# Second feed-forward: eight sums of output weights made in DRAM beside its first product

## The chip, the cores and the metric

The kernel runs on one core of one Trainium2 chip. The metric is the device time of one execution in microseconds. Its engines are TensorE (PE in the profile, with its weight loads as PEld), VectorE (DVE), ScalarE (ACT), GpSimd (POOL) and SyncE (SP), which here only issues DMAs. GpSimd issues DMAs too: those that add to what stands at their destination.

## What is computed

One decoder layer on 512 tokens of width 1024, all in float32. Two feed-forwards stand around a token mixer, each between two RMS norms; the feed-forward's inner width is 2816.

```python
def swiglu_ffn(x, w_in, w_out):
    gate, up = jnp.split(x @ w_in, 2, axis=-1)
    return (jax.nn.silu(gate) * up) @ w_out

x = x + 0.5 * rms_norm(swiglu_ffn(rms_norm(x, norm_pre[l, 0]), ffn1_w_in[l], ffn1_w_out[l]), norm_post[l, 0])
mixed = token_mixer(rms_norm(x, norm_pre[l, 1]), w_mix_in[l], ..., w_mix_out[l])
x = x + rms_norm(mixed, norm_post[l, 1])
x = x + 0.5 * rms_norm(swiglu_ffn(rms_norm(x, norm_pre[l, 2]), ffn2_w_in[l], ffn2_w_out[l]), norm_post[l, 2])
```

The token mixer has two groups of recurrent heads (HGRN2 and mLSTM) that read columns of one projection. The change touches only how one operand of the second feed-forward's second product, `ffn2_w_out`, is prepared.

## The kernel before

**Precision.** Every operand of a large product is split into a high part (a rounded copy) and a low part (what the copy lost), and a product is three passes on TensorE: high by high, high by low, low by high. For a block of weights the split is `split` (line 271): ScalarE makes the high part (line 294), VectorE subtracts it to get the low one (line 296). `feed` (line 332) keeps up to four split blocks ahead of TensorE.

**Stages, in order of time.** The first feed-forward has its first product (`ffn_in`, line 843) and its second (`ffn_out`, line 964); then come the mixers (`mixer`, line 1778, with jobs of projection that fill TensorE between the steps of the recurrences); then the second feed-forward through the same two functions, with `self.second` true.

**Seven products for eight.** Blocks of a feed-forward's first product are multiplied by a scheme of seven products for a 2 by 2 block, so quarters of weights must be added to one another. There are 11 pairs of inner blocks with seven products each (some blocks of the second feed-forward are done ahead in another way). In the first product these sums are made on VectorE (line 310, a few on GpSimd). `ORDER2` is the second feed-forward's order of 76 products, written out by hand; its first 14 are made by `ffn_head`, and `ffn_in` loops over the other 62 with index n. One product is 24 matmuls of 256 columns.

**Loads.** `weights` (line 207) fixes for each load the index at which it is due: when its ring of buffers (`raw`, three deep, or `raw2`, five deep) has a free place, and not more than eight blocks before its first use. `load_due` (line 236) issues it on SP's queue (line 255). SP takes its queue in order, so a load that waits for a buffer holds up whatever stands behind it.

**Sums of the output weights, in DRAM.** In the second product some inner blocks are "quartered", that is also done with seven products for eight: eight of them in the first half of the output columns and five (first feed-forward) or seven (second) in the second half. The sums of output weights that they need are not made on an engine but in DRAM, one item for each quartered block, by `sums_ahead` (line 932). An item is a generator of four steps: three copies from `ffn2_w_out` into a tile `f2sums` on SP's queue, put behind the newest weight load (lines 938 to 940; 128, 128 and 256 KB); then three DMAs of GpSimd that add to the tile (line 944; 256, 128 and 128 KB), one in each step, each waiting for what it reads. The sum is later loaded like a weight.

`sums_due(f, n, done)` (line 947) sets which items are still to do: those from `done` to `n` in the order of the dictionary. `make_sums` (line 956), at each call, starts one more item and takes every started one a step further. So one item takes four calls, and m items take m + 3 calls.

The 15 items of the second feed-forward, before: the copies of the first seven (`EARLY`) are issued at the end of the first feed-forward by `copies_early`, and their adds come in the mixers, behind GpSimd's making of masks. The next six, up to `AHEAD` = 13, are made in the mixers: `job_f` (for `conv0` to `conv3`) and `job_t` (for `hi` and `mv`) call `make_sums` 12 times. The last two are made in the first half of the second product, where `ffn_out` calls `make_sums` after every other block, six times. The first feed-forward makes its own 13 items differently: from n = 15 on in its `ffn_in`, every fifth product (`EVERY`), ten calls, and the rest in `ffn_out`.

The order of instructions on each engine comes from the program's order and a planner's modelled times; `behind` (line 513) ties an instruction behind another one of its engine.

Of the kernel before, what the change touches and what calls it, by code (L numbers as in the profile page):

```python
# [91 lines left out]
PLACES, LATER = {2: 1, 4: 2, 6: 0, 8: 3}, {7: (2, 3)}  # L92

AGAIN, ROWS = (10,), (18, 19, 20, 21)
EVERY, EARLY, AHEAD = 5, 7, 13

# [25 lines left out]
class Layer:  # L124
# [718 lines left out]
    def ffn_in(self):  # L843

        nc = self.nc
        if not self.second:
            self.begun = ()
            self.sums_due("f1")
        for n, (p, t) in enumerate(ORDER2[len(HEADS2) :] if self.second else ORDER[len(HEADS) :]):
            if n > 14 and n % EVERY == 0 and not self.second:  # L850
                self.make_sums()
            if n == 14 and self.second:

                with self.behind(self.pooled):
                    nc.gpsimd.drain()
            with self.behind(*(self.c22 if p in ("p3", "p5") and self.second else ())):
                self.feed()
            self.c22 = []
            self.lag()
            self.prod(p, t)  # L860
            self.after(p, t)
            if t == PAIRS - 1 and p in ("p3", "p7"):
                self.hs.append(self.h_tile(len(self.hs)))
            if n == 1 and not self.second:
                self.lower_bound()
        self.feed()
        self.lag()
# [96 lines left out]
    def ffn_out(self, gpost_row, scale, after, trans, head):  # L964
# [89 lines left out]

        with self.behind(*([self.loaded] if self.second else [])):
            g = self.gain("gpost", gpost_row)
        if self.second:
            self.sums_due("f2", done=AHEAD)
        n = 0
        for half in range(2):  # L1060
            C = [[self.ps() for _ in range(2)] for _ in range(2)]
# [716 lines left out]
    def mixer(self):  # L1778
        nc, tc = self.nc, self.tc
        self.got, self.jobs = set(), deque()  # L1780
        self.sums_due("f2", AHEAD, EARLY)
        with tc.tile_pool(name="ma", bufs=1) as ma:
            self.vh = ma.tile([P, NT, NH, P], F32, name="vh")
            self.qk = ma.tile([P, NT, T], F32, name="qk")
            self.sT = ma.tile([P, 16, P], F32, name="sT")
            self.qd = ma.tile([P, NH, 3 * P], F32, name="qd")
            self.kdt = ma.tile([P, NH, 3 * P], F32, name="kdt")
            self.S = self.kdt.rearrange("p h (c v) -> p h c v", v=P)
            self.eend = ma.tile([P, 16], F32, name="eend")
            with tc.tile_pool(name="mb", bufs=1) as mb:  # L1790
                self.mb = mb
                kes = [mb.tile([P, NT, P], F32, name=f"ke{n}") for n in range(2)]
                self.q = [mb.tile([P, 2, T], F32, tag="q", bufs=2, name=f"q{p}") for p in range(2)]
                self.xr1 = ma.tile([P, 2, D], F32R, tag="vm", bufs=1, name="xr1")
                self.xr = {}
                qps = {}
                for n in range(NH):
                    self.jobs.append(self.job_f(f"hq{n}", lambda ps, n=n: qps.__setitem__(n, ps)))
                for n in range(4):
                    self.jobs.append(self.job_f(f"conv{n}", lambda ps, n=n: self.conv(n, ps)))  # L1800
                self.jobs.append(self.job_rows())
                self.jobs.append(self.job_t("hi", lambda i, ps: nc.scalar.copy(self.vh[:, i].rearrange("p h v -> p (h v)"), ps), self.xr))
                self.jobs.append(self.job_t("mv", lambda i, ps: self.values_mv(ma, i, ps)))

                with tc.issue_after(self.pow.ins):
                    self.gate_weights(ma, mb)
                self.forget_gates(mb)
                with tc.issue_after(self.pow.ins):
                    nc.gpsimd.memset(self.sT, 0.0)
                    self.masks(ma, mb)  # L1810
                self.until("hq3")
                for n in range(NH):
                    nc.scalar.activation(self.q[n // 2][:, n % 2], qps[n], AF.Silu)
                self.hgrn_levels(0, kes, FILL[0])
                self.until("rows")
                nc.scalar.activation(self.qk, self.qk, AF.Silu)
                self.hgrn_levels(1, kes, FILL[1], self.gate_rows(ma))
            with tc.tile_pool(name="mc", bufs=1) as mc:
                self.y = mc.tile([P, NT, D], F32, name="y")
                self.jobs.append(self.job_t("hg", lambda i, ps: nc.scalar.activation(self.y[:, i, :W], ps, AF.Silu)))  # L1820
                self.until("hi")
                self.spread_maxima()
                self.hgrn_states()
                self.mlstm_scores(mc)
                self.jobs.append(self.job_t("mo", self.gate_mo))
                self.chunks(self.mlstm_values, FILL[2])
                self.until("hg")
                self.chunks(self.hgrn_values, FILL[3])
                self.until("mo")
                for i in range(NT):  # L1830
                    self.to_t(i, self.y[:, i], (0,))
                self.mix_out0()
# [145 lines left out]
```

## Time and profile before

| | |
|---|---|
| median of three runs | 915.06 us (914.81 to 915.23) |
| the profiled execution | 914.82 us, span 913.1 us |
| mean granted clock of TensorE | 0.999 |
| HBM read, written | 143.20 MB, 31.48 MB |
| first product of the first feed-forward, about | 12 to 223 us |
| mixers, about | 340 to 585 us |
| first product of the second feed-forward, about | 585 to 800 us |
| its second product, about | 795 to 907 us |

A row of a group gives line, engine, operation, the tile written and the tiles read, shapes, count, and then busy time and mean duration of one; a row of one line or tile gives the shortest, median and longest duration in ns and the first and last start. A wait row gives who waited, for what, and the total in us, the times and the longest. "PEq", "SPq" and so on are the engines' queues, which issue DMAs and wait.

### The profile page before, as it was taken

What the parts mean: (1) busy time and instruction counts of PE and PEld (TensorE: products, weight loads), DVE (VectorE), ACT (ScalarE), POOL (GpSimd) and SP (SyncE); (2) the same over time, 40 slices, a digit from 0 to 9 for tenths busy, and PEclk for the clock granted to TensorE, in tenths of its full rate; (3) what the DMA queues carried; (4) which work ended last, traced back from release to release, by engine and by line L of the source; (5) the groups of instructions that cost most, each with busy time, mean ns of one, the idle gap of its engine ahead of it and who ended that gap; (6) DMA issues with size and microseconds to landing.
All of it is one profiled execution on the core that took longest, in us unless ns stands there. A gap on an engine that the chain in (4) does not pass through costs nothing.

```text
span 913.1 us, 18148 instructions
## 1 busy us (share of the span) xinstructions
PE 904.7 (99%) x7330; PEld 874.7 (96%) x7330; DVE 767.1 (84%) x1005; ACT 522.3 (57%) x749; POOL 183.2 (20%) x256
## 2 busy tenths in 40 slices
PE   9999999999999999999999999999999999999997
PEld 8999999999999999998888888899999999999997
DVE  6899988889888876699986655699899889988886
ACT  7645545557566557857643345694445545757661
POOL 2541112121111047742230300313000000010002
PEclk9999999999999999999999999999999999999999
DMA  9355779775897825899953127053354445388542
GB/s 311 83 161 140 186 191 213 188 156 137 222 273 237 249 62 143 158 200 210 204 119 116 40 76 253 24 162 95 97 156 140 139 130 156 101 238 242 171 144 93
DMA packets 127921, 146.51 MB, mean 160 GB/s; under 512 B 16335, under 2 KB 100303, under 8 KB 127837
## 3 DMA queue, kind: packets, MB, share of 16 engines
q1 hardware_dynamic: 111868, 130.14, 46.8%
q0 software_dynamic: 15680, 14.69, 11.8%
q8 instruction: 57, 0.93, 0.4%
q10 hardware_dynamic: 288, 0.52, 0.2%
q14 instruction: 28, 0.22, 0.1%
HBM read 143.20 MB, written 31.48 MB: 191 GB/s over the span
## 4 chain that ended last, share of the span: by engine, by line
PE 62%; ACT 0%; DVE 0%; DVEq 0%; POOLq 0%; issue 0%; POOL 0%; ACTq 0%
PE ps L619 23%; PE ps L1012 8%; PE ps L549 6%; PE ps L198 5%; PE ps L200 5%; PE ps L199 5%; PE ps L1004 4%; PE ps L560 1%; PE ps L1441 1%; PE ps L364 1%; PE ps L1540 0%; PE ps L1742 0%; PE ps L1491 0%; PE ps L1715 0%; PE ps L1739 0%; PE ps L1505 0%
## 5 line engine op out<-in xcount | busy, mean ns | idle before, releaser
L294 ACT CAST w<-raw 128x1024 fp32r<-128x1024 f32 x246 | 250.9, 1027 | 190.6 <-PE ps L619 91.7
L296 DVE TENSOR_TENSOR w<-raw,w 128x1024 fp32r<-128x1024 f32 x246 | 299.4, 1221 | 30.7 <-ACT w L294 29.5
L619 PE MATMUL ps<-xq,w 128*128 128x256 f32 x2016 | 236.9, 277 | 0.0
L619 PEld LDWEIGHTS ps<-xq,w 128*128 128x128 f32 x2016 | 232.8, 188 | 0.0
L619 PE MATMUL ps<-sq,w 128*128 128x256 f32 x1512 | 177.6, 276 | 0.0
L619 PEld LDWEIGHTS ps<-sq,w 128*128 128x128 f32 x1512 | 174.2, 188 | 0.0
L310 DVE TENSOR_TENSOR raw<-raw,raw 128x1024 f32<-128x1024 f32 x72 | 89.8, 1252 | 7.1 <-DMA raw<-in_ffn_w_in_dram 5.6
L1012 PE MATMUL ps<-w,hs 128*128 128x256 f32 x672 | 80.9, 276 | 0.0
L1004 PE MATMUL ps<-w,hs 128*128 128x256 f32 x672 | 79.2, 276 | 0.0
L1012 PEld LDWEIGHTS ps<-w,hs 128*128 128x128 f32 x672 | 78.3, 188 | 0.0
L1004 PEld LDWEIGHTS ps<-w,hs 128*128 128x128 f32 x672 | 77.5, 188 | 0.0
L198 PE MATMUL ps<-w,xq 128*128 128x512 f32 x176 | 71.1, 404 | 0.0
L200 PE MATMUL ps<-w,xq 128*128 128x512 f32 x176 | 68.9, 392 | 0.0
L199 PE MATMUL ps<-w,xq 128*128 128x512 f32 x176 | 68.6, 390 | 0.0
L944 POOL DMA_DIRECT2D f2sums<-in_ffn_w_out_dram x15 | 20.2, 1522 | 178.6 <-DMA f2sums<-in_ffn_w_out_dram 178.1
L549 PE MATMUL ps<-xq,w 128*128 128x256 f32 x480 | 55.7, 278 | 0.0
L549 PEld LDWEIGHTS ps<-xq,w 128*128 128x128 f32 x480 | 54.9, 188 | 0.5 <-issue 0.5
L884 ACT CAST hs<-hf 128x1024 fp32r<-128x1024 f32 x32 | 33.7, 1053 | 27.4 <-PE ps L1012 19.7
L885 DVE TENSOR_TENSOR hs<-hf,hs 128x1024 fp32r<-128x1024 f32 x32 | 39.1, 1223 | 9.0 <-ACT hs L884 8.4
L944 POOL DMA_DIRECT2D f1sums<-f1sums x26 | 22.0, 847 | 108.6 <-DMA f1sums<-in_ffn_w_out_dram 57.4
L944 POOL DMA_DIRECT2D f2sums<-f2sums x30 | 26.3, 911 | 85.7 <-DMA f2sums<-in_ffn_w_out_dram 44.6
L310 POOL TENSOR_TENSOR raw<-raw,raw 128x1024 f32<-128x1024 f32 x12 | 32.6, 2722 | 40.9 <-DVE w L296 40.7
(263 smaller groups left out, 1234.2 us busy)
## 6 DMA issues: line engine op xcount, KB each, us to landing
raw<-in_ffn_w_in_dram SPq DMA_DIRECT2D x98, 512.0 KB, 4.7
raw<-in_ffn_w_out_dram SPq DMA_DIRECT2D x44, 512.0 KB, 5.5
raw<-in_w_mix_in_dram SPq DMA_DIRECT2D x28, 512.0 KB, 4.7
raw<-f2sums SPq DMA_DIRECT2D x15, 512.0 KB, 5.1
raw<-f1sums SPq DMA_DIRECT2D x13, 512.0 KB, 6.4
raw<-in_w_mix_out_dram SPq DMA_DIRECT2D x8, 512.0 KB, 4.3
f2sums<-in_ffn_w_out_dram SPq DMA_DIRECT2D x30, 128.0 KB, 4.9
f2sums<-in_ffn_w_out_dram SPq DMA_DIRECT2D x15, 256.0 KB, 6.4
```

The source lines that it names most:

```text
L198: mm(ps, sh, mh, start=start, stop=False, **kw)
L199: mm(ps, sh, ml, start=False, stop=False, **kw)
L200: mm(ps, sl, mh, start=False, stop=stop, **kw)
L294: nc.scalar.copy(hi, raw)
L296: self.low = nc.vector.tensor_tensor(lo, raw, hi.bitcast(F32), op=ALU.subtract)
L310: added = (nc.vector if late else nc.gpsimd).tensor_tensor(o, o, c, op=ALU.add)
L549: mm(ps[:, u0:u1], w[:, a, k, :], self.xop(k, b, u0, u1), start=k + n + m == 0, stop=k == ND - 1 and n == 2, skip_group_check=True,)
L619: self.nc.tensor.matmul(ps[:, c], wb[b][:, k, v], left[d][:, k, :], start=first and a + n + k == 0, stop=n == 2 and k == KH - 1, skip_grou ...
L885: self.nc.vector.tensor_tensor(lo, src, hi.bitcast(F32), op=ALU.subtract)
L944: nc.gpsimd.dma_start(to[:, a:b], v, accum_op=ALU.add)
L1004: mm(out, a[kk][:, i * P : (i + 1) * P], w[:, b, kk, QUARTER * v : QUARTER * (v + 1)], start=begin and c == kk == n == 0, stop=kk == 1 and ...
L1012: mm(ps[:, QUARTER * c : QUARTER * (c + 1)], A[a][:, c], B[b], start=begin and c == n == 0, stop=n == 2, skip_group_check=True,)
```

## The change

The six items of the mixers and the two of the second product are all made in the second feed-forward's first product. `ffn_in` calls `make_sums` there too, for n = 10, 15, ..., 60, which are 11 calls for eight items; the mixers' calls stay, for the seven early items, and so do those in `ffn_out`, which find nothing left to start.

```diff
-EVERY, EARLY, AHEAD = 5, 7, 13
+EVERY, EARLY = 5, 7
...
         if not self.second:
             self.begun = ()
-            self.sums_due("f1")
+        self.sums_due(*(("f2", None, EARLY) if self.second else ("f1",)))
         for n, (p, t) in enumerate(ORDER2[len(HEADS2) :] if self.second else ORDER[len(HEADS) :]):
-            if n > 14 and n % EVERY == 0 and not self.second:
+            if n > (9 if self.second else 14) and n % EVERY == 0:
                 self.make_sums()
             if n == 14 and self.second:
...
             g = self.gain("gpost", gpost_row)
-        if self.second:
-            self.sums_due("f2", done=AHEAD)
         n = 0
...
         self.got, self.jobs = set(), deque()
-        self.sums_due("f2", AHEAD, EARLY)
+        self.sums_due("f2", EARLY, EARLY)
```

At n = 14 of that loop GpSimd drains, behind its last add of weights; that line is not touched.

## Prediction before the run

> **What bounds the kernel now.** I read the page's head first, then the list of waits kept to TensorE, then the windows by stage.
>
> ```profile
> span 913.1 us, 18148 instructions
> PE 904.7 (99%) x7330; PEld 874.7 (96%) x7330; DVE 767.1 (84%) x1005; ACT 522.3 (57%) x749; POOL 183.2 (20%) x256
> ```
>
> ```profile
> PE ps L194 <- POOL ones L172: 1.2, 1, 1.2
> PE ps L364 <- DVE xn L754: 0.5, 1, 0.5
> PE ps L619 <- ACT xq L384: 0.2, 1, 0.2
> ```
>
> ```profile
> 60.00:220.00 160.00, 160.00 (x1411) 160.00 (x1410) 143.62 (x155) 86.23 (x109) 26.84 (x28) 1.00 0.74 183
> 340.00:410.00 70.00, 70.00 (x612) 69.52 (x611) 53.98 (x84) 51.48 (x66) 44.19 (x65) 1.00 0.79 167
> 410.00:480.00 70.00, 70.00 (x403) 60.36 (x403) 63.53 (x106) 42.67 (x59) 20.21 (x24) 1.00 0.78 174
> 480.00:590.00 110.00, 109.90 (x601) 92.87 (x600) 69.10 (x144) 48.00 (x92) 20.37 (x42) 1.00 0.32 101
> 590.00:640.00 50.00, 50.00 (x440) 50.00 (x440) 47.16 (x48) 35.77 (x51) 12.40 (x7) 1.00 0.44 133
> 640.00:795.00 155.00, 155.00 (x1368) 155.00 (x1367) 142.90 (x156) 83.04 (x105) 0.00 (x0) 1.00 0.42 128
> 795.00:850.00 55.00, 55.00 (x487) 55.00 (x487) 49.99 (x64) 33.15 (x41) 5.75 (x6) 1.00 0.82 239
> 850.00:913.10 63.10, 56.85 (x502) 56.66 (x500) 48.36 (x67) 30.37 (x58) 6.89 (x20) 0.98 0.39 126
> ```
>
> In the window rows the columns are the stretch and its length, then busy time and instructions of TensorE, its weight loads, VectorE, ScalarE and GpSimd, then the granted clock, the DMA share and GB/s. TensorE is busy 904.7 of 913.1 us. All its waits that the trace names add up to 1.9 us, and the first two lie in the first microseconds of the kernel. Of the rest, 63.10 - 56.85 = 6.25 us lie behind the last matmul. Between, the stages are full at a clock of 1.00: the first feed-forward's first product (60 to 220), the mixers (340 to 590, with 0.10 us open), the second feed-forward's first product (590 to 795) and its second product. So whatever the change takes out of the mixers or the second product is worth at most what TensorE waits there, and the only thing it can do to the time is to make TensorE wait in the first product.
>
> **What is moved.** The rows of the tile that holds the sums, all fifteen items of the second feed-forward:
>
> ```profile
> L944 POOL DMA_DIRECT2D f2sums<-f2sums x30: 812/851/1651, 377.4 to 833.2; - x30
> L938 SPq DMA_DIRECT2D f2sums<-in_ffn_w_out_dram x15: 490/507/597, 305.2 to 813.1; - x15
> L939 SPq DMA_DIRECT2D f2sums<-in_ffn_w_out_dram x15: 491/596/2695, 305.7 to 813.6; - x15
> L940 SPq DMA_DIRECT2D f2sums<-in_ffn_w_out_dram x15: 596/596/1465, 306.4 to 814.2; - x15
> L944 POOL DMA_DIRECT2D f2sums<-in_ffn_w_out_dram x15: 1135/1487/2520, 370.9 to 819.4; - x15
> ```
>
> One item is three copies on SP's queue (0.51 + 0.60 + 0.60 = 1.7 us of issue) and three adds on GpSimd's. Seven items stay where they were. Six leave the mixers and two leave the second product; all eight now start at the calls n = 10, 15, ..., 45 of the first product's loop, and their last add is made at the call n = 60, of eleven calls in all.
>
> **Gain in the mixers.** 18 copies and 18 adds go, with their share of a DMA load of 0.78. TensorE's open time there is 0.10 us, in the stretch after the DMAs. A wait could also hide inside a matmul whose end is modelled:
>
> ```profile
> L198 PE MATMUL ps<-w,xq 128*128 128x512 f32 x176 | 71.1, 404 | 0.0
> L199 PE MATMUL ps<-w,xq 128*128 128x512 f32 x176 | 68.6, 390 | 0.0
> ```
>
> The first of the three passes is 14 ns longer than the second, over 176 of them 2.5 us. That is the upper bound of the gain. I take 0: the third pass has no such excess, so it is nearer to a cost of changing from one group to the next than to a wait for data, and what hid the work stays (other matmuls). **Gain in the second product:** TensorE 55.00 of 55.00 us while those two items were made; nothing, from both sides.
>
> **Cost in the first product.** GpSimd has nothing else to do there, as these two rows of its order of time show: its last add of weights ends at 629.3 us, and the next instruction starts at 804.09.
>
> ```profile
> 626.90 2.41 POOL L310 TENSOR_TENSOR raw<-raw,raw 128x1024 f32<-128x1024 f32 x1 [2.42 <-DVE w L296]
> 804.09 1.25 POOL L944 DMA_DIRECT2D f2sums<-in_ffn_w_out_dram  x1 [174.79 <-DMA f2sums<-in_ffn_w_out_dram]
> ```
>
> So the waits of the moved adds (for the copies, and for the add before) hold up only later adds; the drain at n = 14 stands ahead of them, and the norms that need GpSimd come after 850 us. Cost 0. The sums are read late: the last, of (1, 5), is finished by about 795 us and loaded for the last part of the second half, after 850. Cost 0.
>
> SP's queue and the DMA engines are shared with the weights of the product itself. The nearest row is not far: the first feed-forward does the same beside its own first product, ten items begun from 60 to 220 us, 28 GpSimd DMAs, DMA share 0.74, and TensorE 160.00 of 160.00 us. What it does to a weight load, by the two stretches' rows of the load's line (60 to 220, then 640 to 800):
>
> ```profile
> DMA to landing us min/median/max: 3.7/5.6/9.8
> ```
>
> ```profile
> DMA to landing us min/median/max: 3.5/3.6/5.0
> ```
>
> So a weight load beside such copies and adds lands about 2.0 us later (median), 6.2 us at worst. Who notices? VectorE adds loaded quarters to each other and makes the low parts; between 640 and 795 us it is busy 142.90 of 155.00 us, so 12.1 us are open, against 16.4 of 160 in the first feed-forward. From the waits between 590 and 800:
>
> ```profile
> ACT w L294 <- PE ps L619: 56.2, 45, 1.7
> DVE raw L310 <- DMA raw<-in_ffn_w_in_dram: 5.6, 3, 2.1
> ```
>
> Three times VectorE already waits for a load, 5.6 us in all. With 2.0 us more on each that is 6.0 us, under the 12.1 open. Whether TensorE sees it depends on how far the conversions are ahead of it. ScalarE waited 45 times for TensorE to give up a buffer, so mostly they are a full set of four ahead. The thin places I count out from three views: the chain that ended last, where the long run of line 619 begins with the fourth of the stage's 76 products; the conversions of line 296 done by two times; and three issues of loads on SP's queue. TensorE takes a product in 199.00 / 1752 x 24 = 2.726 us.
>
> ```profile
> 595.65 199.00 PE ps L619 x1752
> ```
>
> ```profile
> 585.40:654.60 69.20, 32.20 (x24) 1.00 0.38 115
> 585.40:682.10 96.70, 45.54 (x35) 1.00 0.42 126
> ```
>
> ```profile
> 654.44 0.37 SPq L255 DMA_DIRECT2D raw<-in_ffn_w_in_dram  x1
> 667.65 0.37 SPq L255 DMA_DIRECT2D raw<-in_ffn_w_in_dram  x1
> 670.65 0.37 SPq L255 DMA_DIRECT2D raw<-in_ffn_w_in_dram  x1
> ```
>
> The 24 conversions done by 654.6 us (two weights were made before this stretch) end with that of loop index n = 11; its product is the 23rd of the long run and starts at 595.65 + 22 x 2.726 = 655.6. Lead 1.0 us, the thinnest place. But the copies of the call n = 10 are put behind the newest load, which by the order of due loads is the last of five due with n = 11, issued at 654.44. Every load that the products up to n = 17 need is ahead of the first copy. After that the 35th conversion (n = 22) is done at 682.1 and its product starts at 595.65 + 33 x 2.726 = 685.6: lead 3.5 us. This is the tightest place that the copies can reach, since by the ring depths and the eight weights of lead in the code no load is due from n = 18 to n = 22: the calls n = 15 and n = 20 both put their copies behind the load of 667.65, six copies, 3.4 us, so the load of 670.65 goes at about 667.65 + 0.4 + 3.4 = 671.5, 0.8 us late, and then lands 2.0 us later: 2.8 us against a lead of 3.5. Cost 0, with 0.7 us to spare; the ends are 0 and, with the longest landing, 0.8 + 6.2 - 3.5 = 3.5 us. I take 0 because the nearest row, the first feed-forward's stage, has it with more items and no wait of TensorE. The other wait for a load, near 744 us, has one triple before it.
>
> [...]
>
> **Sum:** the profiled execution took 914.82 us (1.7 outside its span); 0 from the mixers, 0 from the second product, 0 in the first. The median of the three runs is 915.06. I forecast 914.9.
>
> **Rivals.** *A: a load comes too late behind two triples of copies* (place: the products from n = 22 on, near 682 us; it decides once VectorE's wait for a load there grows from 1.5 by more than the lead of 3.5). For it: VectorE is fuller here than in the first feed-forward, and four conversions in a row have such a lead. Against: the median landing leaves it covered. At the longest landing 914.9 + 3.5 = 918.4, slower.
>
> *B: making descriptors on GpSimd holds up VectorE.* That VectorE and GpSimd can hold each other up is in the trace: beside GpSimd's add at 626.90 a VectorE operation took 3.36 us, not 1.22. The rows of line 296 in the stretches 590 to 640, 640 to 795 and 60 to 220:
>
> ```profile
> L296 DVE TENSOR_TENSOR w<-raw,w x19: 1214/1219/3356, 593.0 to 637.4; 128x1024 fp32r<-128x1024 f32 x19
> L296 DVE TENSOR_TENSOR w<-raw,w x57: 1211/1218/1227, 640.0 to 793.1; 128x1024 fp32r<-128x1024 f32 x57
> L296 DVE TENSOR_TENSOR w<-raw,w x61: 1208/1220/1227, 59.4 to 218.7; 128x1024 fp32r<-128x1024 f32 x61
> L944 POOL DMA_DIRECT2D f1sums<-f1sums x18: 805/812/1325, 75.5 to 200.0; - x18
> L944 POOL DMA_DIRECT2D f1sums<-in_ffn_w_out_dram x10: 1135/1172/1487, 70.3 to 214.3; - x10
> ```
>
> If each of the 24 moved adds blocked VectorE for its length, that is 8 x 1.17 + 16 x 0.81 = 22.3 us, less the 12.1 open: 914.9 + 10.2 = 925.1. Against: beside 28 such DMAs the longest of 61 operations was 1227 ns, the same as beside none. [...]
>
> *C: the mixers held hidden waits,* the 2.5 us above: 912.4, faster. For it: the DMA share of 0.78 there; against: only the first of three passes is longer, and the open time is 0.10 us.
>
> *D: the change does not do what it says,* because the program's order is planned from modelled times and the copies or adds come late, beside the second product again, where they are hidden today: 914.9. Against it: the copies are tied only to a load, and in the second product the first add, at 804.09, came 5 us after the issue of its item's last copy:
>
> ```profile
> 798.41 0.60 SPq L940 DMA_DIRECT2D f2sums<-in_ffn_w_out_dram  x1
> ```
>
> **How the numbers follow.** Forecast 0.81, A 0.10, B 0.02, C 0.04, D 0.03. A measurement of this kernel tells about 0.2% from no change, 1.8 us, so the bounds are 913.2 and 916.9. C alone is faster: 0.04. A and B are slower: 0.12. The rest is within: 0.84. The range takes the forecast and the smaller half of A: from 914.2 (0.1 us of open time in the mixers, and the runs' own spread of 0.4, under 914.8) to 914.9 + half of 3.5 = 916.6.
>
> **What would show it.** Right: GpSimd's DMAs of the sums stop near 410 us and come again from about 658 to 795 us, in eight groups; DMA share near 0.7 from 650 to 795; the mixers' share lower; TensorE full in 640 to 795; landings of weight loads there at 5 to 6 us; VectorE's waits for loads up from 5.6 to some 12 us; line 296 still at 1.22 us. Wrong: a TensorE wait on line 619 for a conversion, most likely near 685 us (A), line 296 above 1.3 us beside the adds (B), or a stage from 340 to 590 that is shorter by over 1 us (C).

## The result, and the profile after

The changed kernel takes 925.12 us (median of four runs, 923.97 to 926.45) against 914.93 us for the kernel before on the same chip (914.67 to 915.23): a ratio of 1.0113, interval 1.0097 to 1.0129. The forecast was 914.9 with a range up to 916.6, so it missed by 10 us.

First the head of the page of after and the first two rows of its list of waits kept to TensorE (who waited for what; total us, times, longest):

```profile
span 922.9 us, 18150 instructions
PE 909.1 (99%) x7330; PEld 878.4 (95%) x7330; DVE 764.6 (83%) x1005; ACT 521.8 (57%) x749; POOL 184.6 (20%) x256
```

```profile
PE ps L619 <- DVE ps L638: 5.6, 2, 4.5
PE ps L194 <- POOL ones L172: 1.2, 1, 1.2
```

The span grew by 9.8 us. The first wait row is new: twice TensorE, in the first product (line 619), waited for a subtraction of VectorE out of PSUM (line 638), once for 4.5 us. Now the windows of after, in the columns of the prediction's window rows: the mixers, the stage of the change, and two pieces of that stage:

```profile
410.00:480.00 70.00, 70.00 (x401) 60.27 (x401) 63.20 (x111) 42.89 (x59) 4.78 (x6) 1.00 0.37 100
640.00:800.00 160.00, 154.43 (x1323) 154.09 (x1322) 137.97 (x148) 78.44 (x99) 22.69 (x24) 0.98 0.69 174
690.80:695.30 4.50, 0.05 (x1) 0.02 (x1) 4.47 (x6) 1.84 (x2) 0.00 (x0) 0.90 0.90 247
695.30:700.00 4.70, 4.69 (x22) 4.70 (x23) 3.75 (x5) 1.43 (x2) 1.17 (x1) 0.50 0.77 227
```

In the mixers the DMA share fell from 0.78 to 0.37, and TensorE is as full as before: the work is gone and nothing was gained. In the stage of the change TensorE stands for the whole of the third row while VectorE is busy for 4.47 of its 4.50 us. In the fourth row TensorE is busy, but with 22 matmuls in 4.70 us, 213 ns each, where 154.69 / 1363 = 113.5 ns were usual; the granted clock is 0.50. The chain that ended last, of after between 640 and 805 us, and then the one row of the chain of before from which that 113.5 comes:

```profile
639.97 45.45 PE ps L619 x400
...
694.55 0.62 DVE ps L638
695.18 0.14 issue
695.31 35.74 PE ps L619 x288
...
747.72 0.62 DVE ps L638
748.34 0.14 issue
748.47 55.93 PE ps L619 x480
```

```profile
639.97 154.69 PE ps L619 x1363
```

Before, TensorE ran through the stage without a break. After, the chain passes twice through line 638. Counted from the starts of the single matmuls against 113.5 ns, the losses are 4.6 us (the stall that ends at 695.3), 2.8 us (the half clock behind it), 1.3 us (a second stall, which ends at 748.5) and 1.35 us (a spacing of some 118 ns for the next 33 us). That is 10.1 us; this execution entered the stage 0.3 us earlier, and 9.8 are left.

Why was the subtraction late? VectorE's order of instructions is the same in both kernels. Its order of time, before and then after (start, duration; in brackets the idle time just before the instruction and what ended it):

```profile
679.63 1.23 DVE L310 TENSOR_TENSOR raw<-raw,raw 128x1024 f32<-128x1024 f32 x1 [1.54 <-DMA raw<-in_ffn_w_in_dram]
...
689.78 0.69 DVE L638 TENSOR_TENSOR ps<-ps,hf 128x512 f32<-128x512 f32 x1
```

```profile
684.32 1.23 DVE L310 TENSOR_TENSOR raw<-raw,raw 128x1024 f32<-128x1024 f32 x1 [6.69 <-DMA raw<-in_ffn_w_in_dram]
...
694.47 0.69 DVE L638 TENSOR_TENSOR ps<-ps,hf 128x512 f32<-128x512 f32 x1
```

The first row of each is an add of two quarters of weights, 5a += 5b, whose result no product before n = 28 needs. It waits for the load of 5b: 1.54 us before, 6.69 us after. The subtraction that TensorE needs for n = 24 stands ten places behind it. It comes 10.15 us after the add in both kernels (689.78 - 679.63 and 694.47 - 684.32), so the whole lateness of a load that no product needed yet is handed on to the subtraction, and through it to TensorE.

SP issued the load of 5b at 674.19 us, even before the 674.65 of the kernel before; it is the longest of the landings. First the rows of that issue and of its landing, then, of after, the landings of the weight loads issued between 640 and 800 us (shortest, median, longest), and VectorE's waits for them between 640 and 805:

```profile
674.19 0.37 SPq L255 DMA_DIRECT2D raw<-in_ffn_w_in_dram  x1
raw<-in_ffn_w_in_dram SPq DMA_DIRECT2D x1, 512.0 KB, 10.0
```

```profile
DMA to landing us min/median/max: 3.7/5.0/10.0
```

```profile
DVE raw L310 <- DMA raw<-in_ffn_w_in_dram: 13.9, 5, 6.7
```

### The profile page after: what moved, and what is told of

It is laid out like the page before. It is cut to its first block, busy times and chain, and to the rows that moved or that the text cites. A ratio compares the mean times of both kernels' runs of the same rounds, so it can differ in the third digit from the quotient of the medians.

```text
span 922.9 us, 18150 instructions
## 1 busy us (share of the span) xinstructions
PE 909.1 (99%) x7330; PEld 878.4 (95%) x7330; DVE 764.6 (83%) x1005; ACT 521.8 (57%) x749; POOL 184.6 (20%) x256
## 4 chain that ended last, share of the span: by engine, by line
PE 60%; DVE 2%; DMA 1%; issue 0%; ACT 0%; DVEq 0%; POOLq 0%; POOL 0%; ACTq 0%
PE ps L619 21%; PE ps L1012 8%; PE ps L549 6%; PE ps L198 5%; PE ps L200 5%; PE ps L199 5%; PE ps L1004 4%; PE ps L560 1%; PE ps L1439 1%; DMA raw<-in_ffn_w_in_dram 1%; PE ps L364 1%; DVE w L296 1%; PE ps L1538 0%; DVE raw L310 0%; PE ps L1740 0%
## 5 line engine op out<-in xcount | busy, mean ns | idle before, releaser
L619 PE MATMUL ps<-sq,w 128*128 128x256 f32 x1512 | 180.9, 279 | 5.6 <-DVE ps L638 5.6
L619 PEld LDWEIGHTS ps<-sq,w 128*128 128x128 f32 x1512 | 177.3, 190 | 5.9 <-issue 4.6
L310 DVE TENSOR_TENSOR raw<-raw,raw 128x1024 f32<-128x1024 f32 x72 | 89.7, 1250 | 15.3 <-DMA raw<-in_ffn_w_in_dram 13.9
L200 PEld LDWEIGHTS ps<-w,xq 128*128 128x128 f32 x176 | 33.0, 188 | 7.4 <-DVE xq L371 0.3
```

Source lines behind the costliest of these rows:

```text
L200: mm(ps, sl, mh, start=False, stop=stop, **kw)
L310: added = (nc.vector if late else nc.gpsimd).tensor_tensor(o, o, c, op=ALU.add)
L619: self.nc.tensor.matmul(ps[:, c], wb[b][:, k, v], left[d][:, k, :], start=first and a + n + k == 0, stop=n == 2 and k == KH - 1, skip_grou ...
```

## The experiments

### What makes the loads late

The first theory was the queue of rival A: loads wait behind copies on SP's own queue (Q). Against it stood GpSimd's adds in DRAM (G), and simply the bytes in the stage, whoever issues them (V).

**e1_spread**: the same eight items, the calls placed so that each triple of copies stands behind another group of loads.

```diff
-            if n > (9 if self.second else 14) and n % EVERY == 0:
+            if n in (10, 15, 21, 27, 33, 39, 44, 49, 52, 55, 58) if self.second else n > 14 and n % EVERY == 0:
```

> The eleven calls are at n = 10, 15, 21, 27, 33, 39, 44, 49, 52, 55, 58, so that no two triples of copies follow one another on SP's queue: each stands behind another weight load. Bytes, adds and copies are the same. Theory Q (a weight load waits its turn behind the copies on SP's own queue, and two triples in a row are too much): VectorE's wait of 6.7 us for a load near 684 us falls under 3 us, TensorE's 4.5 us wait and the half clock behind it go, 915 to 918 us. Theory G (the adds that GpSimd issues take the DMA engines from the loads) and theory V (it is the number of bytes in this stage, whoever issues them): the same bytes, 921 to 925 us.

Measured: 921.78 us, ratio 1.0076 (1.0061 to 1.0091).

**e2_copies_only**: the adds of the eight items are left out.

```diff
-                nc.gpsimd.dma_start(to[:, a:b], v, accum_op=ALU.add)
+                if early or f == "f1":
+                    nc.gpsimd.dma_start(to[:, a:b], v, accum_op=ALU.add)
```

> The eight moved items are copied but nothing is added to them, so those sums of weights are left out; the calls stay at n = 10, 15, ..., 60. Theory Q: the copies alone make the load near 674 us late, 922 to 925 us, with a VectorE wait of over 5 us for it. Theory G: no adds, no late load, 915 to 916 us. Theory V: half the bytes, in between, near 918 us.

Measured: 918.80 us, 1.0043 (1.0028 to 1.0058).

**e3_adds_only**: the copies of all eight are issued in the mixers (in the kernel before, those of six were); only the adds come in the first product, tied to the newest weight block by a copy of one column on GpSimd.

```diff
+                if self.second:
+                    self.mark = nc.gpsimd.tensor_copy(self.col(), self.newest[:, 0, :1])
...
-            with self.behind(*([self.selected] if f == "f2" else [])):
+            with self.behind(*([self.mark if self.second else self.selected] if f == "f2" else [])):
...
```

> The copies of the eight items are issued in the mixers, and only the adds are made in the first product, each call's behind a one-column copy on GpSimd of the newest weight block. Theory Q: nothing on SP's queue ahead of the loads, 915 to 916 us, VectorE's waits for loads under 8 us in all. Theory G: the adds are all there, 921 to 925 us. Theory V: half the bytes, near 918 us.

Measured: 917.55 us (nine runs: five from 916.63 to 917.55, four from 920.36 to 923.03), 1.0049 (1.0028 to 1.0069).

**e4_pool_copies**: GpSimd issues the copies of the eight, at the same calls, so that SP's queue holds only loads there.

```diff
+        late = f == "f2" and not early
+        by = nc.gpsimd if late else nc.sync
+        with self.behind(self.mark if late else last):
+            by.dma_start(to[:, 0], q[:, 0, 1])
...
```

> The copies of the eight items are issued by GpSimd, not by SP, at the same calls, each behind a one-column copy of the newest weight block; the adds follow on the same queue. Same bytes. Theory Q: the loads are alone on their queue, 915 to 917 us. Theory V: the same bytes in the same stage, 921 to 925 us. Theory G: more work on GpSimd's queue, not better than 921 us.

Measured: 926.93 us, 1.0136 (1.0113 to 1.0158). Of these four, the waits of TensorE for line 638, in the order e1, e2, e3, e4, and the loads' landings in e4 (the profiled executions of e3, 920.36 us, and of e4, 930.12, are longer than their medians):

```profile
PE ps L619 <- DVE ps L638: 2.9, 2, 2.3
```

```profile
PE ps L619 <- DVE ps L638: 1.8, 1, 1.8
```

```profile
PE ps L619 <- DVE ps L638: 4.0, 2, 2.6
```

```profile
PE ps L619 <- DVE ps L638: 6.6, 4, 3.8
DMA to landing us min/median/max: 3.7/5.8/8.8
```

Q falls as the account of the whole loss: without a copy on SP's queue (e4) the loads land no sooner at the median and the time is no better, and spreading the copies gives back only a third. At the one load on which the first stall hangs, Q has a share. Of e1, e4 and e2, the load of 5b and its landing, which took 10.0 us in after:

```profile
raw<-in_ffn_w_in_dram SPq DMA_DIRECT2D x1, 512.0 KB, 6.1
```

```profile
raw<-in_ffn_w_in_dram SPq DMA_DIRECT2D x1, 512.0 KB, 6.8
```

```profile
raw<-in_ffn_w_in_dram SPq DMA_DIRECT2D x1, 512.0 KB, 7.6
```

With three copies ahead of its group (e1), with none (e4), or with six but no adds (e2) it lands sooner, and the loss in the stall near 690 us falls from 4.6 us to 0.8 in e1 and 1.6 in e4. But there later stalls are larger than in after, 2.6 us (e1) and 4.1 us (e4) near 745 us. G falls as the only cause: without any add some 4 us of the loss stay. V comes nearest: each half of the traffic alone costs 3 to 4.5 us, both together 10, though e4 is 2 us above what V had expected. But V doesn't say why a late load costs anything, and in all four it is a subtraction of VectorE on the same line, 638, that TensorE waits for.

### Whether the lateness has to cost

The next theory (H): the loads may be late, but they cost only because an add that waits for one stands ahead of the subtraction in VectorE's order. The rival (L): the weights themselves come too late for their products.

**f1_add_later**: the changed kernel, with the same DMAs; the adds of the later groups are tied behind VectorE's last subtraction that opens a bank for a `p6` product.

```diff
-            tt(self.two_by(q), self.two_by(bank["p5", t]), h1, ALU.subtract)
+            self.qsub = tt(self.two_by(q), self.two_by(bank["p5", t]), h1, ALU.subtract)
...
-        with self.behind(*self.hold):
+        with self.behind(*self.hold, *([self.qsub] if it.adds and it.adds[-1][0][0] == "f2" and it.adds[-1][0][1] > 3 else [])):
             for out, other in it.adds:
```

> The changed kernel, with VectorE's first add of each later group (5a += 5b, 9a += 9b, 6a += 6b and so on) ordered behind the last subtraction out of PSUM, so that nothing that waits for a new load stands ahead of the subtraction that TensorE needs. Same loads, same copies, same bytes. Theory H (the late load costs because an add that waits for it stands in VectorE's order ahead of that subtraction): the stall of 4.7 us near 690 and the half clock behind it go, about 7.5 us; what is left is the slower spacing and perhaps a smaller stall near 741: 915 to 919 us. Rival L (the weights themselves come too late for their own products, whatever stands in the order): the wait moves to the product that needs them, at about 700: 923 to 926 us.

Measured: 914.88 us (eleven runs, 914.30 to 915.56), ratio to before 0.9999 (0.9989 to 1.0008). The whole 10 us are gone, more than H had expected, which kept a second stall. Of this kernel: the windows of the stage, of the stretch of the old stall and of the one behind it, the landings of its loads, VectorE's one wait for a load, and the subtraction for n = 24:

```profile
640.00:800.00 160.00, 160.00 (x1413) 160.00 (x1412) 147.93 (x163) 84.34 (x106) 22.74 (x24) 1.00 0.70 184
690.80:695.30 4.50, 4.50 (x42) 4.50 (x42) 4.50 (x6) 2.73 (x4) 2.82 (x3) 1.00 0.98 226
695.30:700.00 4.70, 4.70 (x44) 4.70 (x43) 3.92 (x5) 2.60 (x3) 0.00 (x0) 1.00 0.75 173
```

```profile
DMA to landing us min/median/max: 3.7/4.9/10.7
```

```profile
DVE raw L310 <- DMA raw<-in_ffn_w_in_dram: 2.3, 1, 2.3
```

```profile
688.55 0.70 DVE L638 TENSOR_TENSOR ps<-ps,hf 128x512 f32<-128x512 f32 x1 [1.22 <-PE ps L619]
```

The DMA share is 0.70 as in after, the loads land as late (10.7 us at worst), SP issues the same six copies ahead of the same load. TensorE is full at a clock of 1.00. In the last row VectorE now waits for TensorE: it is ahead again. L falls.

**g1_first_add** ties only 5a += 5b, **g2_other_adds** only the adds of the groups behind it; the edit is that of f1_add_later with the condition `it.adds[-1] == (("f2", 5, "a"), ("f2", 5, "b"))`, and with `> 5` in place of `> 3`.

> The changed kernel with the order of one add alone changed: 5a += 5b behind VectorE's subtraction out of PSUM. If the stall of 4.7 us near 690 and what follows it (half clock 2.9 us) hang on this one add: 7.5 us less, and the second stall near 747 with its slower spacing, 2.7 us, stays: 916.5 to 918.5 us. Rival: the queue comes to its next add and stalls there, 921 us or more. Other rival: the second stall was only a consequence of the first, so that nothing stays: 914.9 us.

> The changed kernel with the adds of the later groups (9, 6, 7, 8, 10) put behind the subtraction, 5a += 5b left where it stands: the first stall and the half clock stay, the second stall goes: 921 to 923.5 us. If all hangs on the first add: 925 us; if the later ones are what matters: 915 to 918 us.

Measured: g1 919.84 us, 1.0060 (1.0048 to 1.0073); g2 921.87 us, 1.0081 (1.0067 to 1.0095). TensorE's wait row of g1, then of g2:

```profile
PE ps L619 <- DVE ps L638: 3.4, 2, 3.0
```

```profile
PE ps L619 <- DVE ps L638: 4.6, 1, 4.6
```

In g2 the first stall stays at its old size and the second is gone, as expected. In g1 the first stall is gone, but what is left is larger than the 916.5 to 918.5 us that were expected: the later wait grew from 1.1 (5.6 - 4.5) to 3.0 us, with some half clock of its own. Most likely a TensorE that had not been stopped at 690 reaches the next such place earlier against its loads; no run tests that. So at least two places of the same kind are at work, and the first covered part of the second.

**g3_before_later**: the kernel before with the edit of f1_add_later.

> The kernel before with the same later adds as f1_add_later: no wait there held TensorE, so no difference, 914.6 to 915.3 us, whichever theory holds. If the later order were worth something by itself, 914 us or less, and then the changed kernel with later adds hides a cost of the same size.

Measured: 914.99 us, 1.0002 (0.9993 to 1.0011). The later order is worth nothing by itself; it only takes the loss away.

**f5_later_spread**: f1_add_later and e1_spread together.

> The changed kernel with both the later adds of VectorE and the triples of copies spread so that each stands behind a load group of its own. Theory H: no stall of over 1 us is left in the first product, 914.5 to 917 us. Rival L: no better than the spread alone, 921 to 923 us.

Measured: 914.90 us, 1.0001 (0.9992 to 1.0010). With the order mended, the place of the copies makes no difference.

### The slack, tried directly

**f2_delay1** and **f3_delay4**: the kernel before with the low part of one block made twice, and five times.

```diff
-            self.low = nc.vector.tensor_tensor(lo, raw, hi.bitcast(F32), op=ALU.subtract)
+            for _ in range(5 if it.key == ("f2", 3, "b") else 1):
+                self.low = nc.vector.tensor_tensor(lo, raw, hi.bitcast(F32), op=ALU.subtract)
```

> The kernel before, with one VectorE instruction near 682 us done twice (the low parts of weight 3b, product 21 of the second feed-forward): 1.13 us more of VectorE's time, no DMA touched. If TensorE's slack against VectorE there is the 0.4 us that the subtraction of the 128x512 PSUM tile shows in the trace of before: a stall of about 0.7 us near 690, time 915.4 to 915.9 us. If the slack is the 3.5 us of the conversions, as the prediction had it: no stall, 914.9 us.

> The kernel before, with the same VectorE instruction done five times: 4.5 us more of VectorE's time there, no DMA touched. By a slack of 0.4 us: a stall of about 4.1 us near 690 and, as behind the 4.7 us stall of the changed kernel, some 3 us lost at half the TensorE clock: 921 to 923 us. By a slack of 3.5 us: a stall of about 1 us, 915.5 to 916.5 us. If the half clock belongs to the transfers and not to the stall: stall of 4.1 us alone, about 919 us.

Measured: f2 915.20 us, 1.0002 (0.9993 to 1.0011); f3 916.83 us, 1.0022 (1.0013 to 1.0031). As a test of the slack at the subtraction both are inconclusive: the planner counted the added work and put other instructions ahead of the late add, so that the subtraction came at 690.53 in f3, hardly later than before. TensorE's wait in f3 is another one (its lines are one higher, by the added line):

```profile
PE ps L620 <- DVE w L297: 1.3, 1, 1.3
```

It waited for the low part itself. Of 4 x 1.13 = 4.5 us of delay (the spacing of such operations on VectorE) some 3 were covered. So the conversions have about the lead that the prediction counted (here that of n = 21, there that of n = 22); it was the lead of the wrong thing.

## Why the prediction was wrong

**Right.** The gain in the mixers and in the second product was 0: in f1_add_later, where the first product costs nothing, the whole change is worth nothing (0.9999). Rival C, hidden waits in the mixers, falls with it. GpSimd's adds cost VectorE nothing, so rival B falls (that such an add is a making of descriptors was its supposition, which no run shows); in after, line 296 took, between 640 and 805 us:

```profile
L296 DVE TENSOR_TENSOR w<-raw,w x57: 1210/1216/1227, 639.7 to 802.9; 128x1024 fp32r<-128x1024 f32 x57
```

The change does what it says (D falls): the DMA share in the stage is 0.69, near the 0.7 foretold. Even the lateness was sized well at the median: the loads land at 5.0 us where 5.6 had been taken, and VectorE's waits for loads rose to 13.9 us where some 12 had been foretold. That this sum came out is partly luck: 2 us more on each of three waits had been taken, and one wait alone grew to 6.7 us.

**The step that failed** is "Whether TensorE sees it depends on how far the conversions are ahead of it", with the lead of 3.5 us at n = 22 set against 2.8 us of lateness. The lead was counted at line 296 alone. But TensorE also waits for line 638, the subtraction out of PSUM, and in VectorE's order that stands ten places behind the add and started 10.15 us after it in both kernels. By the row of before the subtraction ends at 689.78 + 0.69 = 690.47; product n = 24 is the 36th of the long run and starts at 595.65 + 35 x 2.726 = 691.06. The lead there is 0.6 us (0.45 after the 0.14 us of issue that the chain of after shows), and the add ten places ahead was already waiting for a load. The right question was not how early the late load's own product is, but which instruction, somewhere behind the waiting one in the same queue, is needed first. VectorE's 12.1 us of open time in the stage were no cover either, since none of it lies between the waiting add and the subtraction. The two views that tell it were both at hand, VectorE's waits and its order of time; the prediction used only the first.

**The size of the lateness at that place.** 2.8 us were taken, from medians, with 0.8 + 6.2 as the worst. The add began 684.32 - 679.63 = 4.7 us later, and all of it by the landing of 10.0 us: the 0.8 us behind the copies fell on the load of 5a, issued at 671.42 as foretold, not on that of 5b. Even the 2.8 would have cost over 2 us through a lead of 0.6, so the lead is the error and this is the smaller one.

**The nearest row misled.** The first feed-forward has the same copies and adds beside its first product and no wait of TensorE, and from this the cost of 0 was taken. Its loads do land late, at 5.6 us. But these are all of VectorE's waits that the trace names between 60 and 220 us, in before:

```profile
DVE ps L638 <- PE ps L619: 11.0, 10, 1.4
DVE w L296 <- ACT w L294: 3.5, 12, 0.5
DVE hf L638 <- PE ps L619: 0.4, 1, 0.4
```

No load is among them: there VectorE waits for TensorE and ScalarE. The second feed-forward had three waits for loads, 5.6 us, before anything was moved. The row had the same traffic, but there the late loads were still early enough for VectorE, and whether they are was the question.

**What was not priced.** A stall was taken to cost its own length. The half clock behind the first added 2.8 us to stalls of 4.6 + 1.3, and a slower spacing behind the second, whose cause is open, 1.35.

**Rival A** had the right place (a load near 682 us that comes late) and half of the mechanism; its price, 3.5 us, was the worst landing less the wrong lead. The six copies ahead on SP's queue fit the late landing of the load of 5b but don't settle the time. That load took 10.0 us behind six copies, 6.1 behind three (e1) and 6.8 with none on SP's queue (e4); yet e1 and e4 still lost 7 and 12 us, and in e4 the median landing was 5.8 us, no sooner. How much of the 10 us is the order in the queue and how much the bytes stays open: without adds the same six copies gave 7.6 us (e2), so copies and adds both do a part of it.

## What to carry to other kernels

When transfers are put beside a stage, don't ask only whether the late data's own user has time: look in the order of every engine that waits for that data for the first instruction behind the waiting one that the bounding engine needs, and count its lead. A stage "that does the same and is full" is a witness only if its engines wait for the same things; compare the wait rows, not only the traffic. And where such a lead is thin, the cheap remedy is the order: an add that isn't needed for four products, put behind a subtraction that is needed now, took 10 us of loss to nothing at the same DMA traffic.

## What the runs showed of the hardware

**A stall can cost TensorE more than its length.** Behind the stall of 4.7 us the granted clock was 0.50 and a matmul took 213 ns until about 701 us, some 27 matmuls and 2.8 us of loss. f1_add_later, with the same traffic and no stall, has a clock of 1.00 in that stretch, so it belongs to the stall. By the starts of the matmuls, the half rate also came behind the stalls of 3.2 us in g1 (clock 0.59 from 744.70 to 746.50), 4.1 us in e4 and 4.9 us in g2 (0.64 from 695.80 to 700.00), and ended 3.1 to 3.7 us after them; it ended 5.9 us after the 4.7 us stall of the changed kernel. Shorter ones went both ways: behind 2.1 us (e2) and 2.6 us (e1) there were 1.5 and 1.7 us of such loss, behind 2.8 us (e3) none (the mean clock from 640 to 800 us was 0.99 in e2 and in e1, 1.00 in e3), and none behind any of 1.7 us or less.

**A third rate.** After the second stall matmuls came 118 ns apart, not 113.5, until about 782 us, at a granted clock shown as 1.00. The windows of before and of after show it in the number of matmuls:

```profile
748.50:782.00 33.50, 33.50 (x297) 33.50 (x297) 31.41 (x36) 18.10 (x25) 0.00 (x0) 1.00 0.47 142
```

```profile
748.50:782.00 33.50, 33.50 (x284) 33.50 (x285) 29.44 (x32) 15.53 (x20) 4.50 (x5) 1.00 0.81 204
```

g2_other_adds shows the same spacing from about 700 to 720 us, behind its stall (349 matmuls in the 40 us from 700, against 352 at 113.5 ns), and after did not have it there (337 in the 38 us from 702, against 335). It does not belong to the moved transfers: f3_delay4, where no DMA was moved, has it too, behind its stall of 1.6 us. From 685.80 us, first in before, then in f3:

```profile
685.80:715.50 29.70, 29.70 (x264) 29.70 (x263) 28.02 (x30) 15.39 (x20) 0.00 (x0) 1.00 0.46 142
```

```profile
685.80:715.50 29.70, 29.70 (x254) 29.70 (x254) 28.43 (x31) 15.40 (x19) 0.00 (x0) 1.00 0.52 158
```

Nor does every stall bring it: behind the 2.6 us of e1 the matmuls were 113.5 ns apart again. TensorE is shown as busy throughout, and nothing in the trace names the cause; it stays open.
